# Feed-forward input of a hybrid attention/mLSTM block: one plain step fewer, one seven-product step more, and two weight sums per step formed by accumulating DMA

## The chip, the cores and the metric

The kernel runs on one core of a Trainium2 chip, in fp32 kept exact enough by splitting. The metric is device time in microseconds (us) of one execution; a run is given as the median of its executions. TensorE (PE) multiplies, VectorE (DVE) and ScalarE (ACT) do elementwise work and empty PSUM, GpSimd (POOL) does small work and issues DMAs in software, SyncE (SP) issues most DMAs.

## The reference

Two layers on 512 tokens of width 1024: a dilated attention mixer and an mLSTM mixer, each followed by a SwiGLU feed-forward. The change is in the feed-forward's first half, run once per layer:

```python
def swiglu(xn, w_in, w_out):
    gu = xn @ w_in
    return (jax.nn.silu(gu[..., :D_FF]) * gu[..., D_FF:]) @ w_out
```

`xn` is the RMS-normalized activation, 512 x 1024; `w_in` is 1024 x 5632 (gate and up, D_FF = 2816 columns each); `w_out` is 2816 x 1024.

## The kernel before

**Split products.** TensorE takes operands in a reduced format (float32r). Each fp32 operand is split into a high half, rounded by ACT (`split_chunk`, line 208), and a low half, the remainder, by DVE (line 209). Each product is then three matmuls (`SPLITS`: high-high, high-low, low-high).

**Steps.** `ffn_in` works through the 2816 hidden columns in eleven steps of 256 (j = 0, 2, ..., 20), each step making gate and up of its columns for all 512 tokens. There are two kinds.

A plain step (`plain`, `multiply`, line 239) multiplies four weight chunks of 512 x 256 in the usual way: 96 matmuls that are 512 wide. The normalization factor is multiplied in when PSUM is emptied (line 959).

A product step (`weights_of`, `products`, line 1017) uses a seven-product scheme in the manner of Strassen and Winograd. The weights of a step are four blocks, A11 and A12 (gate, first and second half of the input rows) and A21 and A22 (up), 512 KB each; the tokens are blocks B11 to B22 of the normalized input. From them come the sums S1 to S4 (weights) and T1 to T4 (tokens), and seven products of 256 x 512 x 256 replace eight: `PRODUCTS` lists them in order. Each is 24 matmuls that are 256 wide, so a step has 168. The token sums are made once per layer by the generator `normalized` and kept as split tiles; `some(n)` runs its next n pieces. The weight sums are made in each step by DVE (`total`, line 988) when a block has been split (`prepare`, line 992):

```python
                if key == "A11":
                    total("S1", "A21", "A22", ALU.add, "own")
                elif key == "S1":
                    total("S2", "S1", "A11", ALU.subtract, "own")
                elif key == "S2":
                    total("S3", "A11", "A21", ALU.subtract, "A21")
                elif key == "A12":
                    total("S4", "A12", "S2", ALU.subtract, "A12")
```

S1 and S2 share one buffer (tag `t1`), S3 overwrites A21, S4 overwrites A12.

**Buffers and order.** Splitting runs two products ahead of TensorE (`AHEAD`). Split halves have three buffers each (`whi`, `wlo`), A22 and A12 three (`wraw`), A11 and A21 lie together in a tile of tag `w8` with two buffers; the two `w8` buffers first hold the normalized tokens. A scheduler sets the order of instructions on each engine and the waits by data and buffer dependence; an engine and a DMA queue take their instructions in that order, so an instruction that waits holds up all behind it. All weight loads are issued from SP (line 980). Pool issues nothing in this stage.

In the trace the stage's tiles are named `f0...` and `f1...` by layer; buffer numbers are left out, so `f0j8S` is the S1 and S2 buffer of step j8 and `f0j10A` its neighbour's A blocks; `f0j_w` is a `w8` tile. `_h` and `_l` are the high and low halves.

Of the kernel before, what the change touches and what calls it, by code (L numbers as in the profile page):

```python
# [11 lines left out]
F32 = mybir.dt.float32  # L12
# [3 lines left out]
ALU = mybir.AluOpType  # L16
AX = mybir.AxisListType
P = 128

SEQ = 512  # L20
# [50 lines left out]
def tile_hybrid_dilated_attn_mlstm(  # L71
# [4 lines left out]
    nc = tc.nc  # L76
# [268 lines left out]
    with ExitStack() as actx:  # L345
# [16 lines left out]
        ang, n, sn, cs = (tmp[:, 0, i * P:(i + 1) * P] for i in range(4))  # L362
# [430 lines left out]
        def out_project(pairs, w2d, nk, name, first=0, end=KC // 2):  # L793
            for c in range(first, end):
# [4 lines left out]
        acc = [[acc_tile("awo0_%d" % m) for m in range(2)],  # L799
               [ps.tile([P, 512], F32, tag="s", name="awo1_%d" % m, bufs=2) for m in range(2)],  # L800
               [acc_tile("awo2_0"), ps.tile([P, 512], F32, tag="t", name="awo2_1", bufs=1)]]
# [51 lines left out]
    HALF = SEQ // 2  # L853

    PRODUCTS = (("A11", "B11"), ("S1", "T1"), ("S2", "T2"), ("A12", "B21"), ("S3", "T3"), ("S4", "B22"), ("A22", "T4"))
    PLAIN = 6
    AHEAD = 2

    def ffn_in(layer, fp, pair, rbc, hook, following):
# [11 lines left out]
        def place(i, name, dtype):  # L871
            p, tag = (xp, "x%d" % (i - 3)) if 3 <= i < 11 else (fp, "hid%d" % i)
            return p.tile([P, 2, SEQ], dtype, tag=tag, name="f%d%s%d" % (layer, name, i))
# [1 line left out]
        def hidden(i):  # L875
            return place(i, "hid", F32)

        def temp(tag, name, bufs=1):
            return fp.tile([P, SEQ], F32, tag=tag, name=name, bufs=bufs)

        def op_tile(i, name):
            return fp.tile([P, 4, HALF], F32R, tag="op%d" % i, name="f%d%s" % (layer, name))
# [4 lines left out]
        def split_tokens(key):  # L887
            i = [b for _, b in PRODUCTS].index(key)
            hi, lo = ops[key] = [op_tile(2 * i + part, key + "hl"[part]) for part in range(2)]
            nc.scalar.activation(hi, raw[key], AF.Copy)  # L890
            nc.vector.tensor_tensor(lo, raw[key], hi.bitcast(F32), op=ALU.subtract)

        def normalized():
            xs = [fp.tile([P, 4, SEQ], F32, tag="w8", name="f%dx%d" % (layer, i), bufs=2) for i in range(2)]
            for i in range(2):
                for t in range(2):
                    raw["B%d%d" % (i + 1, t + 1)] = xs[i][:, :, t * HALF:(t + 1) * HALF]
            for k in range(KC):
                nc.vector.scalar_tensor_tensor(xs[k // 4][:, k % 4], h[k], col("ffn", layer * KC + k), rbc,
                                               op0=ALU.mult, op1=ALU.mult)  # L900
                yield
            split_tokens("B11")
            raw["T1"] = fp.tile([P, 4, HALF], F32, tag="t1", name="f%dt1" % layer)
            nc.vector.tensor_tensor(raw["T1"], raw["B12"], raw["B11"], op=ALU.subtract)
            yield

            raw["T3"] = raw["B12"]
            nc.vector.tensor_tensor(raw["T3"], raw["B22"], raw["B12"], op=ALU.subtract)
            split_tokens("T1")
            yield  # L910
            split_tokens("T3")
            yield
            split_tokens("B22")
            yield
            raw["T2"] = raw["B22"]
            nc.vector.tensor_tensor(raw["T2"], raw["B22"], raw["T1"], op=ALU.subtract)
            split_tokens("T2")
            yield
            split_tokens("B21")
            yield  # L920

            raw["T4"] = raw["B21"]
            nc.vector.tensor_tensor(raw["T4"], raw["B21"], raw["T2"], op=ALU.subtract)
            split_tokens("T4")

        hid = []
        steps = normalized()
        STEPS = 2

        def some(n):  # L930
            for _ in itertools.islice(steps, n):
                pass
# [10 lines left out]
        def plain(j):  # L943
            nm = "f%dj%d" % (layer, j)
            acc = {(half, m): bank("%s_%d%d" % (nm, half, m)) for half in range(2) for m in range(2)}
            gates = {}
            hid.append(hidden(j // 2))
            for ch in range(KC // 4):
                for half in range(2):
                    whl = ready.pop(0)  # L950
                    split_next()
                    for m in range(2):
                        multiply(acc[half, m], whl, pair, ch, m, KC)
                        if j == 0 and (ch, half, m) == (1, 0, 0):
                            hook()
                    if ch == KC // 4 - 1:
                        for m in range(2):
                            t = temp("gu%d" % half, nm + "gu", 3 - half)
                            nc.vector.tensor_tensor(t, acc[half, m], rbc, op=ALU.mult)
                            if half == 0:  # L960
                                nc.scalar.activation(t, t, AF.Silu)
                                gates[m] = t
                            else:
                                nc.vector.tensor_tensor(hid[-1][:, m], t, gates[m], op=ALU.mult)
                    advance()
                    if j > 0 or ch == 1:
                        some(STEPS)


        def weights_of(j):  # L970

            nm = "f%dj%d" % (layer, j)
            w8 = fp.tile([P, 2, 1024], F32, tag="w8", name=nm + "_w8", bufs=2)
            w = {"A11": w8[:, 0], "A21": w8[:, 1]}
            for key in ("A22", "A12"):
                w[key] = wp.tile([P, 1024], F32, tag="wraw", name=nm + key, bufs=W_BUFS)
            for key in ("A11", "A22", "A12", "A21"):
                half, ch = int(key[1]) - 1, int(key[2]) - 1
                c0 = half * D_FF + j * P
                nc.sync.dma_start(w[key].rearrange("p (k n) -> p k n", k=4),  # L980
                                  wi[ch * 4 * P:(ch + 1) * 4 * P, c0:c0 + 256].rearrange("(k p) n -> p k n", p=P))

            def split(key):
                return split_chunk((w[key], 1024, lambda t: t.rearrange("p (k n) -> p k n", k=4), nm + key))

            def total(key, a, b, op, place):
                w[key] = w[place]
                nc.vector.tensor_tensor(w[key], w[a], w[b], op=op)
            w["own"] = fp.tile([P, 1024], F32, tag="t1", name=nm + "S")
            made = {}  # L990

            def prepare(key):
                made[key] = split(key)

                if key == "A11":
                    total("S1", "A21", "A22", ALU.add, "own")
                elif key == "S1":
                    total("S2", "S1", "A11", ALU.subtract, "own")
                elif key == "S2":
                    total("S3", "A11", "A21", ALU.subtract, "A21")  # L1000
                elif key == "A12":
                    total("S4", "A12", "S2", ALU.subtract, "A12")
            return [(lambda key=key: prepare(key)) for key, _ in PRODUCTS], made

        def products(j, made):
# [44 lines left out]
            def p3():  # L1050
                product("S4", "B22", "p5", fresh=False)
                hid.append(hidden(j // 2))
                t["g2"] = temp("gu0", nm + "g2", 3)
                add(t["g2"], acc["p5"], t["u2"])
                nc.scalar.activation(t["g2"], t["g2"], AF.Silu)
                nc.vector.tensor_tensor(hid[-1][:, :, HALF:], first(t["v5"]), first(t["g2"]), op=ALU.mult)

            def p4():
                product("A22", "T4", "u", fresh=False)
                nc.vector.tensor_tensor(hid[-1][:, :, :HALF], first(acc["u"]), first(t["g1"]), op=ALU.mult)  # L1060
            return [p1, p5, p6, p2, p7, p3, p4]

        split_next()
# [6 lines left out]
        def prepare(n):  # L1070
            if n < len(todo):
                j, i = todo[n]
                if j not in prepared:
                    prepared[j] = weights_of(j)
                prepared[j][0][i]()
            else:
                out_weights.append(following(n - len(todo)))
# [12 lines left out]
                part.append(x)  # L1090
        for n in range(AHEAD):
            prepare(n)
        some(None)
        for n, (j, i) in enumerate(todo):
            prepare(n + AHEAD)
            if i == 0:
                steps_of = products(j, prepared[j][1])
            steps_of[i]()
            if i % 2:
                advance()  # L1100
            if n >= len(todo) - 3:
                split_hidden()
# [305 lines left out]
    with ExitStack() as fctx:  # L1408
# [3 lines left out]
        def load(ch, n):  # L1412
            src = wo[ch * 2 * P:(ch + 1) * 2 * P, n * 512:(n + 1) * 512].rearrange("(k p) n -> p k n", p=P)
            return split_weights(src, [P, 2, 512], "fw%d_%d" % (n, ch))
# [127 lines left out]
```

## Time and profile before

| what | us |
|---|---|
| median of three runs (1428.53 to 1429.28) | 1428.57 |
| profiled execution's own time | 1428.88 |
| its span, first to last instruction | 1427.1 |
| TensorE busy | 1415.9 (99%) |
| DVE busy | 960.4 (67%) |
| ACT busy | 603.4 (42%) |
| Pool busy | 84.8 (6%) |
| feed-forward input, layer 0: three plain steps | 503.7 to 570.4 |
| feed-forward input, layer 0: eight product steps | 570.4 to 731.7 |

The span is one execution taken by the hardware profiler. Busy times of matmuls overlap, since they are pipelined; what a matmul costs is the distance between the starts of two of them. In rows of the windows the columns are the stretch in us, its length, and for each engine its busy time and the number of instructions, then the granted TensorE clock, the share of the DMA engines and GB/s. In rows of the timeline they are start, duration, engine, line, operation, tile written and tiles read, and in brackets the idle time before it with what ended that. In rows of the DMA issues the last number is the median time from issue to landing.

### The profile page before, as it was taken

How to read it: one execution, taken by the hardware profiler on the slowest of the kernel's cores; microseconds unless marked ns; L12 is line 12 of the kernel's file. 1: busy time of each engine (PE TensorE's matmuls, PEld its weight loads, DVE VectorE, ACT ScalarE, POOL GpSimd, SP SyncE). 2: the span in 40 equal slices, each digit the busy share in tenths (PEclk: the TensorE clock that was granted, in tenths of full speed). 3: DMA queues.
4: the chain of work that ended last, by engine and by line, in shares of the span. 5: the costliest groups of instructions: out<-in, count | busy, mean ns of one | idle time of the engine just before them, and what ended most of it. 6: DMA issues, size and time to landing. Idle time of an engine off the chain costs nothing. (4 is left out here: it accounts for less than half of the span.)

```text
span 1427.1 us, 20255 instructions
## 1 busy us (share of the span) xinstructions
PE 1415.9 (99%) x7986; PEld 1241.2 (87%) x7986; DVE 960.4 (67%) x1679; ACT 603.4 (42%) x1009; POOL 84.8 (6%) x137
## 2 busy tenths in 40 slices
PE   9999999999999999999999999999999999999998
PEld 7888888888888888999998888888888899998887
DVE  7857567567567397787782358897758777888233
ACT  5333224224225353444462233696534354445123
POOL 1011011011002000000000010110000000001001
PEclk9999999999999999999999999999999999999999
DMA  6346236235335434323233232321133332346331
GB/s 193 102 115 201 75 104 191 97 108 151 133 104 145 145 101 133 107 72 118 90 96 96 96 98 74 104 60 60 55 113 96 122 118 83 96 118 180 116 106 72
DMA packets 133688, 158.67 MB, mean 111 GB/s; under 512 B 7060, under 2 KB 121044, under 8 KB 133592
## 3 DMA queue, kind: packets, MB, share of 16 engines
q1 hardware_dynamic: 125616, 131.55, 29.6%
q0 software_dynamic: 6320, 24.69, 6.2%
q8 instruction: 63, 1.03, 0.3%
q10 hardware_dynamic: 1656, 1.12, 0.2%
q14 instruction: 33, 0.27, 0.1%
HBM read 143.18 MB, written 14.16 MB: 110 GB/s over the span
## 5 line engine op out<-in xcount | busy, mean ns | idle before, releaser
L1471 PE MATMUL fin<-fw_l,f1hh 128*128 128x512 f32 (+1 forms) x198 | 72.5, 366 | 0.0
L1471 PE MATMUL fin<-fw_h,f1hh 128*128 128x512 f32 (+1 forms) x198 | 72.4, 366 | 0.0
L1471 PE MATMUL fin<-fw_h,f1hl 128*128 128x512 f32 (+1 forms) x198 | 72.4, 365 | 0.0
L209 DVE TENSOR_TENSOR fo_k_l<-fo_k_w,fo_k_h 128x1024 fp32r<-128x1024 f32 (+1 forms) x24 | 27.2, 1135 | 62.0 <-ACT fo_k_h L208 62.0
L239 PE MATMUL fo<-f0hh,fo_k_h 128*128 128x512 f32 x176 | 68.5, 389 | 0.0
L239 PE MATMUL fo<-f0hl,fo_k_h 128*128 128x512 f32 x176 | 68.5, 389 | 0.0
L239 PE MATMUL fo<-f0hh,fo_k_l 128*128 128x512 f32 x176 | 68.5, 389 | 0.0
L209 DVE TENSOR_TENSOR fw_l<-fw_w,fw_h 128x1024 fp32r<-128x1024 f32 x22 | 27.1, 1233 | 59.9 <-ACT fw_h L208 59.9
L208 ACT ACTIVATE fo_k_h<-fo_k_w 128x1024 fp32r<-128x1024 f32 (+1 forms) x24 | 23.7, 989 | 74.7 <-PE fo L239 74.7
L208 ACT ACTIVATE fw_h<-fw_w 128x1024 fp32r<-128x1024 f32 x22 | 23.3, 1060 | 67.6 <-PE fin L1471 67.0
L1471 PEld LDWEIGHTS fin<-fw_l,f1hh 128*128 128x128 f32 x198 | 37.4, 189 | 6.2 <-DVE fw_l L209 0.2
L1471 PEld LDWEIGHTS fin<-fw_h,f1hh 128*128 128x128 f32 x198 | 37.3, 189 | 6.2
L1471 PEld LDWEIGHTS fin<-fw_h,f1hl 128*128 128x128 f32 x198 | 37.3, 188 | 6.0
L239 PEld LDWEIGHTS fo<-f0hh,fo_k_l 128*128 128x128 f32 x176 | 33.0, 188 | 6.9
L239 PEld LDWEIGHTS fo<-f0hl,fo_k_h 128*128 128x128 f32 x176 | 33.0, 188 | 6.9
L239 PEld LDWEIGHTS fo<-f0hh,fo_k_h 128*128 128x128 f32 x176 | 33.0, 188 | 6.7
L239 PE MATMUL f0j<-n_h,f0j_h 128*128 128x512 f32 x96 | 37.5, 390 | 0.0
L239 PE MATMUL f1j<-n_h,f1j_h 128*128 128x512 f32 x96 | 37.5, 390 | 0.0
L239 PE MATMUL f0j<-n_h,f0j_l 128*128 128x512 f32 x96 | 37.4, 389 | 0.0
L239 PE MATMUL f1j<-n_h,f1j_l 128*128 128x512 f32 x96 | 37.4, 389 | 0.0
L239 PE MATMUL f0j<-n_l,f0j_h 128*128 128x512 f32 x96 | 37.3, 389 | 0.0
L239 PE MATMUL f1j<-n_l,f1j_h 128*128 128x512 f32 x96 | 37.3, 389 | 0.0
(2105 smaller groups left out, 4886.0 us busy)
## 6 DMA issues: line engine op xcount, KB each, us to landing
f0j_w<-in_ffn_w_in_dram SPq DMA_DIRECT2D x28, 512.0 KB, 4.9
f1j_w<-in_ffn_w_in_dram SPq DMA_DIRECT2D x28, 512.0 KB, 4.4
fw_w<-in_ffn_w_out_dram SPq DMA_DIRECT2D x22, 512.0 KB, 3.9
fo_k_w<-in_ffn_w_out_dram SPq DMA_DIRECT2D x20, 512.0 KB, 3.5
awo_k_w<-in_attn_w_out_dram SPq DMA_DIRECT2D x8, 512.0 KB, 7.1
mv_k_w<-in_mlstm_w_in_dram SPq DMA_DIRECT2D x8, 512.0 KB, 3.7
mqk_k_w<-in_mlstm_w_in_dram SPq DMA_DIRECT2D x8, 512.0 KB, 3.9
mo_k_w<-in_mlstm_w_in_dram SPq DMA_DIRECT2D x8, 512.0 KB, 3.7
```

The costliest lines, as they stand in the source:

```text
L208: nc.scalar.activation(hi[:, :n], raw[:, :n], AF.Copy)
L209: nc.vector.tensor_tensor(lo[:, :n], raw[:, :n], hi[:, :n].bitcast(F32), op=ALU.subtract)
L239: nc.tensor.matmul(acc, whl[a][:, k, m * P:(m + 1) * P], pairs[b][kk], start=(kk == 0 and (a, b) == SPLITS[0]), stop=(kk == nk - 1 and (a, ...
L1471: nc.tensor.matmul(acc[i][:, cs], a[a_][kk][:, tb * P:(tb + 1) * P], whl[b_][:, k, cs], start=(kk == 0 and (a_, b_) == SPLITS[0]), stop=(k ...
```

## The change

`PLAIN` goes from 6 to 4: each layer has two plain steps (j = 0, 2) and nine product steps (j = 4 to 20).

The signs of the scheme are turned so that every weight sum is an addition, the up blocks counting as negative: S1 = A21 + A22, S2 = S1 + A11, S3 = A11 + A21, S4 = A12 + S2, with T1, T2 and T4 turned to match, and a factor -1 in the last multiplication of a step.

S1 and S3 are no longer made by DVE. SP loads A11 twice, once into its place and once into S3's; Pool loads A21 into S1's buffer and then issues two DMAs that add to what lies there: A22 onto S1, A21 onto S3. S2 and S4 stay on DVE.

The token sums' pieces come in another order; what is left of them after the plain steps runs one piece per product in the first product step. T1 has a tile of its own (`tt`), and the first product step's A11 and S3 lie in two buffers of the normalized input, since the tokens still hold the `w8` tiles.

```diff
-    PLAIN = 6
+    PLAIN = 4
...
-            w8 = fp.tile([P, 2, 1024], F32, tag="w8", name=nm + "_w8", bufs=2)
-            w = {"A11": w8[:, 0], "A21": w8[:, 1]}
+
+            if j == PLAIN:
+                w8 = [place(i, nm + "_w8", F32).rearrange("p a b -> p (a b)") for i in (5, 6)]
+            else:
+                w8 = fp.tile([P, 2, 1024], F32, tag="w8", name=nm + "_w8", bufs=2)
+                w8 = [w8[:, 0], w8[:, 1]]
+            w = {"A11": w8[0], "S3": w8[1], "S1": fp.tile([P, 1024], F32, tag="t1", name=nm + "S")}
             for key in ("A22", "A12"):
                 w[key] = wp.tile([P, 1024], F32, tag="wraw", name=nm + key, bufs=W_BUFS)
-            for key in ("A11", "A22", "A12", "A21"):
-                half, ch = int(key[1]) - 1, int(key[2]) - 1
+
+            def load(key, block, engine, **kw):
+                half, ch = int(block[1]) - 1, int(block[2]) - 1
                 c0 = half * D_FF + j * P
-                nc.sync.dma_start(w[key].rearrange("p (k n) -> p k n", k=4),
-                                  wi[ch * 4 * P:(ch + 1) * 4 * P, c0:c0 + 256].rearrange("(k p) n -> p k n", p=P))
+                engine.dma_start(w[key].rearrange("p (k n) -> p k n", k=4),
+                                 wi[ch * 4 * P:(ch + 1) * 4 * P, c0:c0 + 256].rearrange("(k p) n -> p k n", p=P), **kw)
+            for key, block in (("A11", "A11"), ("S3", "A11"), ("A22", "A22"), ("A12", "A12")):
+                load(key, block, nc.sync)
+
+            load("S1", "A21", nc.gpsimd)
+            load("S1", "A22", nc.gpsimd, accum_op=ALU.add)
+            load("S3", "A21", nc.gpsimd, accum_op=ALU.add)
...
                 made[key] = split(key)
 
-                if key == "A11":
-                    total("S1", "A21", "A22", ALU.add, "own")
-                elif key == "S1":
-                    total("S2", "S1", "A11", ALU.subtract, "own")
-                elif key == "S2":
-                    total("S3", "A11", "A21", ALU.subtract, "A21")
+                if key == "S1":
+                    total("S2", "S1", "A11", "S1")
                 elif key == "A12":
-                    total("S4", "A12", "S2", ALU.subtract, "A12")
+                    total("S4", "A12", "S2", "A12")
...
-                nc.vector.tensor_tensor(hid[-1][:, :, HALF:], first(t["v5"]), first(t["g2"]), op=ALU.mult)
+                nc.vector.scalar_tensor_tensor(hid[-1][:, :, HALF:], first(t["v5"]), -1.0, first(t["g2"]),
+                                               op0=ALU.mult, op1=ALU.mult)
...
-        some(None)
         for n, (j, i) in enumerate(todo):
             prepare(n + AHEAD)
+            some(1)
```

In the changed program Pool's queue holds, step after step: the S3 sum of a later step, the A21 load into the S1 buffer, the A22 accumulation onto it.

More of the change, by code (lines that the diff above doesn't have):

```diff
@@ L876, in hidden, with temp @@
             return place(i, "hid", F32)
-        def temp(tag, name, bufs=1):
-            return fp.tile([P, SEQ], F32, tag=tag, name=name, bufs=bufs)
+        def temp(tag, name, bufs=1, shape=[P, SEQ]):
+            return fp.tile(shape, F32, tag=tag, name=name, bufs=bufs)
         def op_tile(i, name):
@@ L901, in normalized @@
                 yield
+            raw["T1"] = temp("tt", "f%dt1" % layer, shape=[P, 4, HALF])
+            nc.vector.tensor_tensor(raw["T1"], raw["B11"], raw["B12"], op=ALU.subtract)
             split_tokens("B11")
-            raw["T1"] = fp.tile([P, 4, HALF], F32, tag="t1", name="f%dt1" % layer)
-            nc.vector.tensor_tensor(raw["T1"], raw["B12"], raw["B11"], op=ALU.subtract)
             yield
-            raw["T3"] = raw["B12"]
-            nc.vector.tensor_tensor(raw["T3"], raw["B22"], raw["B12"], op=ALU.subtract)
             split_tokens("T1")
             yield
-            split_tokens("T3")
+            raw["T3"] = raw["B11"]
+            nc.vector.tensor_tensor(raw["T3"], raw["B22"], raw["B12"], op=ALU.subtract)
+            raw["T2"] = raw["B12"]
+            nc.vector.scalar_tensor_tensor(raw["T2"], raw["T1"], -1.0, raw["B22"], op0=ALU.mult, op1=ALU.subtract)
             yield
[L913 to L916, printed above, removed]
             split_tokens("T2")
@@ L920, in normalized @@
             yield
+            split_tokens("T3")
             raw["T4"] = raw["B21"]
-            nc.vector.tensor_tensor(raw["T4"], raw["B21"], raw["T2"], op=ALU.subtract)
+            nc.vector.scalar_tensor_tensor(raw["T4"], raw["T2"], -1.0, raw["B21"], op0=ALU.mult, op1=ALU.subtract)
+            yield
+            split_tokens("B22")
+            yield
             split_tokens("T4")
@@ L927, in ffn_in @@
         steps = normalized()
-        STEPS = 2
         def some(n):
@@ L966, in plain, with total @@
                     if j > 0 or ch == 1:
-                        some(STEPS)
+                        some(2)
         def weights_of(j):
             nm = "f%dj%d" % (layer, j)
-            w8 = fp.tile([P, 2, 1024], F32, tag="w8", name=nm + "_w8", bufs=2)
-            w = {"A11": w8[:, 0], "A21": w8[:, 1]}
+            if j == PLAIN:
[4 more added lines that the diff above has]
+            w = {"A11": w8[0], "S3": w8[1], "S1": fp.tile([P, 1024], F32, tag="t1", name=nm + "S")}
             for key in ("A22", "A12"):
                 w[key] = wp.tile([P, 1024], F32, tag="wraw", name=nm + key, bufs=W_BUFS)
-            for key in ("A11", "A22", "A12", "A21"):
-                half, ch = int(key[1]) - 1, int(key[2]) - 1
+            def load(key, block, engine, **kw):
+                half, ch = int(block[1]) - 1, int(block[2]) - 1
                 c0 = half * D_FF + j * P
-                nc.sync.dma_start(w[key].rearrange("p (k n) -> p k n", k=4),
-                                  wi[ch * 4 * P:(ch + 1) * 4 * P, c0:c0 + 256].rearrange("(k p) n -> p k n", p=P))
+                engine.dma_start(w[key].rearrange("p (k n) -> p k n", k=4),
[5 more added lines that the diff above has]
+            load("S3", "A21", nc.gpsimd, accum_op=ALU.add)
             def split(key):
                 return split_chunk((w[key], 1024, lambda t: t.rearrange("p (k n) -> p k n", k=4), nm + key))
-            def total(key, a, b, op, place):
+            def total(key, a, b, place):
                 w[key] = w[place]
-                nc.vector.tensor_tensor(w[key], w[a], w[b], op=op)
-            w["own"] = fp.tile([P, 1024], F32, tag="t1", name=nm + "S")
+                nc.vector.tensor_tensor(w[key], w[a], w[b], op=ALU.add)
             made = {}
@@ L1055, in p3 @@
                 nc.scalar.activation(t["g2"], t["g2"], AF.Silu)
-                nc.vector.tensor_tensor(hid[-1][:, :, HALF:], first(t["v5"]), first(t["g2"]), op=ALU.mult)
+                nc.vector.scalar_tensor_tensor(hid[-1][:, :, HALF:], first(t["v5"]), -1.0, first(t["g2"]),
+                                               op0=ALU.mult, op1=ALU.mult)
             def p4():
                 product("A22", "T4", "u", fresh=False)
-                nc.vector.tensor_tensor(hid[-1][:, :, :HALF], first(acc["u"]), first(t["g1"]), op=ALU.mult)
+                nc.vector.scalar_tensor_tensor(hid[-1][:, :, :HALF], first(acc["u"]), -1.0, first(t["g1"]),
+                                               op0=ALU.mult, op1=ALU.mult)
             return [p1, p5, p6, p2, p7, p3, p4]
```

## The prediction

> **What bounds the kernel now.** I read the page's first part, then the windows of single steps, then the timelines of DVE, ACT and SP inside one step, and last the DMA issues. The page first:
>
> ```profile
> span 1427.1 us, 20255 instructions
> PE 1415.9 (99%) x7986; PEld 1241.2 (87%) x7986; DVE 960.4 (67%) x1679; ACT 603.4 (42%) x1009; POOL 84.8 (6%) x137
> ```
>
> TensorE never rests, so only matmul time can be won, and a wait is paid where it reaches TensorE. Busy time misleads for matmuls: the rows give 389 ns for a 512-wide and 283 ns for a 256-wide one, but their starts lie 0.227 and 0.120 us apart. The windows are cut at the first matmuls of four steps of layer 0: plain j2, plain j4, products j6, products j8 (columns: stretch, length, then busy us and count per engine, granted clock, DMA share, GB/s).
>
> ```profile
> 526.89:548.65 21.76, 21.76 (x97) 18.02 (x96) 21.64 (x24) 11.43 (x12) 0.00 (x0) 1.00 0.49 155
> 548.65:570.41 21.76, 21.76 (x97) 18.02 (x96) 13.21 (x14) 5.40 (x6) 0.00 (x0) 1.00 0.32 102
> 570.41:590.57 20.16, 20.16 (x170) 20.15 (x169) 15.15 (x15) 9.88 (x12) 0.00 (x0) 1.00 0.35 106
> 590.57:610.73 20.16, 20.16 (x171) 20.16 (x170) 15.71 (x16) 9.88 (x12) 0.00 (x0) 1.00 0.34 105
> ```
>
> A plain step is 96 matmuls x 0.2267 = 21.76 us, a product step 168 x 0.120 = 20.16 us, both without a gap. Pool does nothing here.
>
> **What TensorE gains.** Each layer trades one plain step for one product step: 21.76 - 20.16 = 1.60 us, for two layers 3.2 us. That is all there is to win: 0.22% of 1428.6 us, just past the 0.2% (2.86 us) that a measurement of this kernel can tell from no change.
>
> **The edits beside TensorE.** Two DVE sums of 1.23 us leave each product step (S1 and S3), so DVE falls from 15.7 to about 13.3 us of 20.16; no gain, TensorE covers it. The two multiplications by -1 (scalar_tensor_tensor, 0.70 us on line 899 against 0.69 for the plain multiplication) cost nothing for the same reason. Preparing the operands in two plain steps: in the second one DVE is full already (21.64 of 21.76), and now products follow at once. I laid the changed order of DVE's queue on the durations above: low half of A11 ready at 546.1 for a product that starts at 548.65, S1 at 547.1 for 551.5, S2 at 551.4 for 554.4, A12 at 554.3 for 557.3. The A11 of the first product step lands in a buffer of the normalized input that TensorE frees at 537.5, and two loads of 5 us fit before. So this costs nothing; with one DVE operation more in front of S2 it would still fit. SP issues four loads a step as before (a second A11 takes the place of A21).
>
> **The new chain through Pool.** This is where the change can lose. S1 has one buffer (tag t1), in which S2 is formed too and which is read until S4 = A12 + S2 is done. Before, DVE rebuilt S1 right after that, in 1.23 us. Now Pool waits for S4, loads A21 into the buffer, waits for the landing, and adds A22 by a second DMA; behind these in Pool's queue stand the S3 sum of a later step and the next S1. The first row below is S4 of step j8, the others are step j10's S1 split, S2 sum, S2 split, A12 split and S4 sum on DVE:
>
> ```profile
> 595.93 1.23 DVE L988 TENSOR_TENSOR f0j8A<-f0j8A,f0j8S 128x1024 f32<-128x1024 f32 x1
> ...
> 609.02 1.23 DVE L209 TENSOR_TENSOR f0j10S_l<-f0j10S,f0j10S_h 128x1024 fp32r<-128x1024 f32 x1 [0.28 <-ACT f0j10S_h L208]
> ...
> 610.76 1.22 DVE L988 TENSOR_TENSOR f0j10S<-f0j10S,f0j_w 128x1024 f32<-128x1024 f32 x1
> ...
> 613.19 1.23 DVE L209 TENSOR_TENSOR f0j10S_l<-f0j10S,f0j10S_h 128x1024 fp32r<-128x1024 f32 x1 [0.61 <-ACT f0j10S_h L208]
> 614.83 1.23 DVE L209 TENSOR_TENSOR f0j10A_l<-f0j10A,f0j10A_h 128x1024 fp32r<-128x1024 f32 x1 [0.41 <-ACT f0j10A_h L208]
> 616.09 1.22 DVE L988 TENSOR_TENSOR f0j10A<-f0j10A,f0j10S 128x1024 f32<-128x1024 f32 x1
> ```
>
> The ACT half of the S1 split starts the chain; the A12 half waits 0.57 us for a buffer that TensorE frees:
>
> ```profile
> 607.93 1.06 ACT L208 ACTIVATE f0j10S_h<-f0j10S 128x1024 fp32r<-128x1024 f32 x1 [1.82 <-PE f0j_p L1017]
> ...
> 613.74 1.06 ACT L208 ACTIVATE f0j10A_h<-f0j10A 128x1024 fp32r<-128x1024 f32 x1 [0.57 <-PE f0j_c L1017]
> ```
>
> From the S1 split's start to S4's end it is 617.31 - 607.93 = 9.4 us, or 8.9 when the chain is late and that buffer is already free. Call the two DMAs, from issue to landing, together Z. Add 0.4 us for each Pool start (0.3 from DVE's end at 121.35 to Pool's issue at 121.65; 0.55 from a landing to the issue at 136.38) and 0.1 to ACT. One round of the chain is Z + 0.9 + 8.9 = Z + 9.8 us, and it fits into a step while Z is at most 20.16 - 9.8 = 10.36.
>
> The first round has more room. From S4's end at 597.16 to the split at 607.93 there are 10.8 us, and S2's low half, done at 614.42, is wanted at 610.73 + 2 x 2.88 = 616.49: 2.0 us of slack. The first product step's S1 is loaded early. Eight rounds follow in each layer, one with the room of 12.8 and seven that repeat: the loss of a layer is (Z + 0.9 - 12.8) + 7 x (Z - 10.36) = 8Z - 84.4, if positive.
>
> **The size of Z.** No accumulating DMA is in this trace. The nearest issues, in us to landing:
>
> ```profile
> ht<-hD POOLq DMA_DIRECT2D x2, 1024.0 KB, 6.8
> a1pT<-a1pD POOLq DMA_DIRECT2D x2, 960.0 KB, 7.3
> a3pT<-a3pD POOLq DMA_DIRECT2D x2, 960.0 KB, 9.0
> f0j10A<-in_ffn_w_in_dram SPq DMA_DIRECT2D x2, 512.0 KB, 4.8
> f0j12A<-in_ffn_w_in_dram SPq DMA_DIRECT2D x2, 512.0 KB, 6.2
> f0j18A<-in_ffn_w_in_dram SPq DMA_DIRECT2D x2, 512.0 KB, 5.7
> a1v<-a1vD POOLq DMA_DIRECT2D x1, 512.0 KB, 4.3
> ```
>
> The load of A21 has the shape of a1v, also from Pool: 4.3 us with little beside it. In the product steps it competes with SP's loads, which there take 4.8 to 6.2; I take 5.4, between them. The accumulation brings 512 KB and reads 512 KB more; from below it costs a plain load, 4.3, from above the slowest transfer of 960 KB, 9.0. I take 6.8, the row of 1024 KB from Pool's queue, since the doubled read is what it is nearest to. Z = 12.2, between 8.6 and 15.2. A cost below a plain load is excluded: the same 512 KB come from memory.
>
> DMA work is the reason not to take the low end. Four loads make a share of 0.34 of 20.16 us, 1.7 us each; with seven loads and two second reads it is 9 x 1.7 = 15.3 us, a share of 0.76.
>
> **The sum.** 8 x 12.2 - 84.4 = 13.2 us a layer, 26.4 for both, less 3.2: 23.2 us slower. Against the profiled execution's own 1428.88 us (1.78 beside its span of 1427.1; 0.31 above the median of 1428.57) that is 1452.1, against the median 1451.8. I forecast 1452.
>
> **The rivals.** *The chain fits.* With Z up to 10.5 (the accumulation near 5 us) ACT finds S1 landed, TensorE stays the bound, and the two layers give their 3.2 us: 1425.4. For it: a load of this shape takes 4.3 us, and even two of them make 8.6. Against it: the second read and SP's four loads, which fall into the same half of the step (issues at 599.6 to 604.5, S4 done at 597.2). Chance 0.21.
>
> *Late by little.* The second read costs only its transfer: 4.3 + 1.7 = 6.0, Z = 11.4, 6.8 us a layer, 13.6 - 3.2 = 10.4 us slower: 1439. Its low edge, Z from 10.6 to 11.0, is no measurable change. Chance 0.15, of which 0.05 within 0.2%. The Trainium skill, Collectives: The Full Stack, section on the bandwidth ceiling, says that a DMA's add costs no cycles of its own and is slower only because two source reads share one ring. By that the time would be this rival's, 1439, and not 1452; no run here shows an accumulating DMA yet.
>
> *Far later.* The read-modify-write is not pipelined as a copy is, and Z passes 15.2: from 1500 us up (Z = 20 would be 75.6 us a layer, 1577). For it: nothing in this trace shows such a transfer at all. Against it: all plain ones of 512 KB land within 6.2 us. Chance 0.12.
>
> **How the numbers follow.** The forecast, Z from 11.5 to 15.2, has the remaining 0.52. Chances: faster 0.21 (the chain fits), same 0.05 (the low edge of late by little), slower 0.10 + 0.52 + 0.12 = 0.74. The range reaches from the fitting chain, 1425, to Z = 15.2, 1500, and leaves out the far case. The likely cases' own range, without the fitting chain, is 1430 to 1500.
>
> **What would show it.** Right: product steps from the second on longer than 20.16 us, by about 1.8 us each, with ACT's S1 split ending its idle time on a Pool DMA and TensorE idle before S1 or S2 products; the first product step and the plain steps without gaps; Pool's accumulating DMAs landing 6 to 9 us after issue. The chain fits: 20.16 us in every product step and S1 landed before ACT asks. Wrong altogether: gaps in the first product step (operand preparation), or a wait on the S3 sum or on SP's loads in place of S1.

## The result

The changed kernel takes 1479.52 us (median of four runs, 1477.29 to 1482.34) against 1428.91 for the kernel before beside it: 50.6 us more, a ratio of 1.0355, 95% interval 1.0337 to 1.0373. Forecast was 1452. The profiled execution took 1477.29 us.

The head of the page after:

```profile
span 1475.5 us, 20650 instructions
PE 1431.5 (97%) x8130; PEld 1256.6 (85%) x8130; DVE 930.7 (63%) x1653; ACT 609.2 (41%) x1021; POOL 144.8 (10%) x191
```

TensorE is at 97% instead of 99%: for the first time it waits. The windows of layer 0, cut at the first matmuls of the product steps j4, j6, j8 and j10 (columns as before):

```profile
549.00:569.15 20.15, 20.15 (x170) 20.15 (x168) 13.01 (x14) 8.30 (x10) 4.62 (x4) 1.00 0.90 225
569.15:595.05 25.90, 23.37 (x171) 22.88 (x169) 13.35 (x13) 9.75 (x12) 3.37 (x3) 0.87 0.56 139
595.05:618.08 23.03, 20.81 (x170) 20.31 (x169) 13.35 (x13) 9.67 (x12) 3.33 (x3) 1.00 0.64 158
618.08:640.56 22.48, 20.67 (x170) 20.26 (x169) 13.34 (x13) 9.67 (x12) 3.33 (x3) 1.00 0.67 162
```

The first product step has no gap, and the second plain step before it still takes 21.76 us, so the hurried operand preparation costs nothing. From the second product step on every step is late, by 1.5 to 5.7 us in layer 0. DVE has the 13.35 us that were forecast. The nine product steps of a layer take 205.1 and 209.1 us.

The new chain, in the timelines of Pool and ACT between step j8's S4 and step j10's. Pool first: load of A21 onto S1, accumulation of A22, the S3 accumulation of another step, the next S1:

```profile
606.31 0.78 POOL L985 DMA_DIRECT2D f0j10S<-in_ffn_w_in_dram  x1 [13.59 <-DVE f0j8A L999]
611.04 1.27 POOL L985 DMA_DIRECT2D f0j10S<-in_ffn_w_in_dram  x1 [3.95 <-DMA f0j10S<-in_ffn_w_in_dram]
614.22 1.27 POOL L985 DMA_DIRECT2D f0j_w<-in_ffn_w_in_dram  x1 [1.91 <-DMA f0j_w<-in_ffn_w_in_dram]
628.79 0.78 POOL L985 DMA_DIRECT2D f0j12S<-in_ffn_w_in_dram  x1 [13.29 <-DVE f0j10A L999]
```

```profile
619.36 1.06 ACT L208 ACTIVATE f0j10S_h<-f0j10S 128x1024 fp32r<-128x1024 f32 x1 [5.89 <-DMA f0j10S<-in_ffn_w_in_dram]
```

In brackets stand the idle time before each instruction and what ended it. Pool waits 13.59 us for DVE's S4 sum; ACT, which found S1 ready before, now waits 5.89 us for the accumulation to land. In most late steps TensorE then waits in the product of S1 and again before that of S2, here in j8 (the rows of its timeline that have an idle time):

```profile
599.25 0.39 PE L1023 MATMUL f0j_p<-f0T1h,f0j8S_l 128*128 128x256 f32 x1 [0.76 <-DVE f0j8S_l L209]
...
603.59 0.39 PE L1023 MATMUL f0j_u<-f0T2h,f0j8S_h 128*128 128x256 f32 x1 [1.46 <-ACT f0j_u L1035]
```

The first wait is for the low half of S1. The second is for a copy on ACT, which stands behind the late splits in ACT's queue.

Z is the time of the load and the accumulation together, from issue to landing, as in the prediction. The DMA lines of two tiles tell its size. Each has two issues, so the minimum is the load and the maximum the accumulation; first f0j4S, the S1 of the first product step, loaded before the stage, then f0j10S:

```profile
DMA to landing us min/median/max: 4.0/5.1/6.3
...
DMA to landing us min/median/max: 4.4/6.3/8.2
```

Over the 16 late rounds of both layers the load takes 4.77 us on average and the accumulation 8.62 (7.0 to 9.8). The rest of a round is as forecast: 8.88 us from the S1 split to S4's end in every round, and 0.93 us of hand-offs in most.

What the DMA engines do during three accumulations, windows from issue to landing of the S1 accumulations of j4, j10 and j12:

```profile
487.24:493.53 6.29, 6.29 (x29) 5.22 (x28) 3.58 (x5) 3.12 (x5) 1.33 (x1) 1.00 0.57 85
611.04:619.25 8.21, 8.21 (x71) 8.21 (x70) 3.41 (x4) 1.09 (x2) 2.55 (x2) 1.00 1.14 279
633.28:642.93 9.65, 9.65 (x83) 9.65 (x82) 3.65 (x4) 1.33 (x2) 2.55 (x2) 1.00 1.15 269
```

The last two numbers of a row are the DMA share and GB/s. The early accumulation is nearly alone. In the late ones the share is over 1, so the engines are full: SP's loads of A22 and A12 and Pool's S3 accumulation lie in the same stretch. Averaged over the step the share is only 0.6 to 0.7, which hides this.

### The profile page after: what moved, and what is told of

The parts are those of the page before. It is cut to its first block, busy times and chain, and to the rows that moved or that the text cites. A ratio compares the mean times of both kernels' runs of the same rounds, so it can differ in the third digit from the quotient of the medians.

```text
span 1475.5 us, 20650 instructions
## 1 busy us (share of the span) xinstructions
PE 1431.5 (97%) x8130; PEld 1256.6 (85%) x8130; DVE 930.7 (63%) x1653; ACT 609.2 (41%) x1021; POOL 144.8 (10%) x191
## 5 line engine op out<-in xcount | busy, mean ns | idle before, releaser
L538 DVE TENSOR_TENSOR rot<-rot,sinr 32x1024 f32<-32x1024 f32 x24 | 28.9, 1205 | 0.0
L239 PE MATMUL mo<-n_h,mo_k_h 128*128 128x512 f32 x64 | 25.5, 399 | 0.0
L239 PE MATMUL mo<-n_h,mo_k_l 128*128 128x512 f32 x64 | 25.2, 394 | 0.0
L239 PE MATMUL mo<-n_l,mo_k_h 128*128 128x512 f32 x64 | 25.1, 393 | 0.0
L239 PE MATMUL mqk<-n_h,mqk_k_h 128*128 128x512 f32 x64 | 25.1, 393 | 0.0
L239 PE MATMUL mqk<-n_l,mqk_k_h 128*128 128x512 f32 x64 | 25.1, 392 | 0.0
```

The source lines that it names most:

```text
L239: nc.tensor.matmul(acc, whl[a][:, k, m * P:(m + 1) * P], pairs[b][kk], start=(kk == 0 and (a, b) == SPLITS[0]), stop=(kk == nk - 1 and (a, ...
L538: nc.vector.tensor_tensor(sh, sh, sinr.unsqueeze(1).to_broadcast([R, 2, SEQ]), op=ALU.mult)
```

## The experiments

The theory: the loss is the chain through the one S1 buffer, whose round is Z + 9.8 us, and Z is too long. The rivals: the DMA work by itself, the two-step operand preparation, and the lower granted clock in j6 (0.87 above). A gap is, here and below, the distance between the starts of two matmuls of TensorE where it is more than the usual 0.120 us.

**Both sums back on DVE.** The two plain steps alone are kept:

```diff
-            for key, block in (("A11", "A11"), ("S3", "A11"), ("A22", "A22"), ("A12", "A12")):
+            for key, block in (("A11", "A11"), ("S3", "A21"), ("A22", "A22"), ("A12", "A12")):
...
-            load("S1", "A21", nc.gpsimd)
-            load("S1", "A22", nc.gpsimd, accum_op=ALU.add)
-            load("S3", "A21", nc.gpsimd, accum_op=ALU.add)
...
+                if key == "A11":
+                    total("S1", "S3", "A22", "S1")
...
+                elif key == "S2":
+                    total("S3", "A11", "S3", "S3")
```

> One part of the change alone: two plain steps and nine product steps, but both weight sums back on DVE (SP loads A21 in S3's place; S1 = A21 + A22 and S3 = A11 + A21 are DVE sums, no Pool DMA in the product steps). Theory A (the whole loss is the chain S4, load, accumulation, S1 through Pool): every product step 20.15 us and plain steps 21.76, one plain step for one product step in each layer, 1428.9 - 3.2 = 1425.7 us. Theory B (preparing the operands in two plain steps also costs something that the late sums hid in the changed kernel): gaps in the first product step or in the second plain step, 1427 us or more. Theory C (the load on DVE: 15.7 us of 20.16 a step already before) would give gaps in all product steps, over 1430 us.

Measured 1426.47 us (11 runs) against 1429.29, ratio 0.9981 (0.9972 to 0.9990): 2.8 us faster, where 3.2 were expected. Windows of its first two product steps:

```profile
548.21:568.36 20.15, 20.15 (x169) 20.15 (x168) 18.96 (x20) 10.83 (x13) 0.00 (x0) 1.00 0.49 157
568.36:588.52 20.16, 20.16 (x170) 20.16 (x169) 15.85 (x16) 9.88 (x12) 0.00 (x0) 1.00 0.34 105
```

No gap, even with DVE at 18.96 us in the first. Only in the last product step of layer 1 is there a small one, of 0.87 us, that the kernel before does not have; it is more than the 0.4 us that are missing, which lie within the interval. The traded step and the operand preparation are what the prediction said; theories B and C fall.

**Two places for S1.** The same DMAs and bytes as the changed kernel, but S1 alternates between the `t1` and `tt` places:

```diff
-"S1": fp.tile([P, 1024], F32, tag="t1", name=nm + "S")
+"S1": fp.tile([P, 1024], F32, tag="tt" if (j - PLAIN) % 4 else "t1", name=nm + "S")
```

> All of the changed kernel, but S1's buffer alternates between two places (the t1 place and the place of T1, free by then): same DMAs, same bytes, same accumulations, only the reuse is one step later. Theory A (the wait for the one buffer, not the DMA work): a round of load and accumulation has two steps, 40.3 us, against Z of 13.4 plus 9.8, so no gaps: 1425.7 us. Rival 1 (the accumulating DMAs are too slow or too many for the queue or the memory): S1 accumulation 7.0 to 9.8 plus load 4.4 plus S3 accumulation 8 us follow one another in Pool's queue, about 20 to 22 us a step: 1428 to 1455 us, with the gaps at S1 or S3. Rival 2 (only the first round's queue order, S3 of j8 ahead): gain of some 10 us alone, 1470.

Measured 1426.35 us, ratio 0.9981 (0.9972 to 0.9990). Windows of its first three product steps:

```profile
549.05:569.20 20.15, 20.15 (x170) 20.15 (x168) 14.88 (x16) 9.88 (x12) 4.65 (x4) 1.00 1.07 254
569.20:589.36 20.16, 20.16 (x171) 20.16 (x169) 13.53 (x14) 9.89 (x12) 3.32 (x3) 1.00 0.76 184
589.36:609.52 20.16, 20.16 (x171) 20.16 (x169) 13.53 (x14) 9.88 (x12) 3.34 (x3) 1.00 0.75 185
```

The DMAs are hardly quicker (Z is 13.1 us on average against 13.4, accumulations 6.9 to 9.6), the share is the 0.76 that was estimated, and no step of layer 0 is late (in layer 1 only the last, by 0.69 us, with the small gap of the run above). So the wait for the buffer is the whole loss of 53 us, and the DMA work costs nothing by itself. This kernel and the one with both sums on DVE are the two that beat the kernel before.

**S1's accumulation alone undone.** Pool still loads A21 into the one buffer, DVE adds A22:

```diff
-            load("S1", "A22", nc.gpsimd, accum_op=ALU.add)
...
+                if key == "A11":
+                    total("S1", "S1", "A22", "S1")
...
```

> S1's accumulating DMA alone undone: Pool still loads A21 into the one S1 buffer after S4, but A22 is added there by DVE (1.23 us); S3 is still an accumulating DMA. Theory A (the chain's length decides, and the accumulation of 7.0 to 9.8 us is the piece that is too long): a round is 0.55 + 4.4 + 0.1 + 1.23 + 8.9 = 15.2 us, below the step of 20.16, so all product steps 20.15 us, 1425.7. Rival (the traffic of Pool's accumulations holds up the loads, wherever they are): S3's accumulation still in every step, loads of 5.5 to 6.5 us, steps of 20.5 to 22, 1432 to 1455. In both the S3 accumulation shows its time to landing with one accumulation less in the queue: under 7 us if the two held each other up, near 8 if it is its own cost beside SP's loads.

Measured 1431.30 us, ratio 1.0013 (1.0004 to 1.0021). Theory A's 1425.7 is missed by 5.6 us, though the chain now fits: rounds are 20.16 us in most steps. The gaps (1.1 to 1.6 us, two in a layer, beside the small one at the end of layer 1) come from DVE's queue, here its timeline in step j8:

```profile
597.94 1.23 DVE L209 TENSOR_TENSOR f0j8S_l<-f0j_w,f0j8S_h 128x1024 fp32r<-128x1024 f32 x1
604.17 1.23 DVE L998 TENSOR_TENSOR f0j10S<-f0j10S,f0j10A 128x1024 f32<-128x1024 f32 x1 [5.01 <-DMA f0j10S<-in_ffn_w_in_dram]
605.32 1.22 DVE L209 TENSOR_TENSOR f0j8S_l<-f0j8A,f0j8S_h 128x1024 fp32r<-128x1024 f32 x1
```

The sum waits 5.01 us for Pool's load, and the low half of S4, which TensorE wants, stands behind it. S3's accumulations took 7.2 us on average, between the two values expected.

**S3's accumulation alone undone.**

```diff
-            for key, block in (("A11", "A11"), ("S3", "A11"), ("A22", "A22"), ("A12", "A12")):
+            for key, block in (("A11", "A11"), ("S3", "A21"), ("A22", "A22"), ("A12", "A12")):
...
-            load("S3", "A21", nc.gpsimd, accum_op=ALU.add)
...
+                elif key == "S2":
+                    total("S3", "A11", "S3", "S3")
```

> S3's accumulating DMA alone undone (SP loads A21 in S3's place, DVE adds A11 after S2; SP's and Pool's loads are one fewer), S1 still by load and accumulation in one buffer, so the chain stays. If S1's accumulation of 8.6 us (mean) is its own cost: Z 13.0, steps from the second product on about 22.8 us, 1470 to 1478 us. If it is slowed by S3's accumulation and its load in the same time: accumulation near the 6.1 to 6.3 us that it takes alone in the first product step's S1, Z = 4.4 + 6.2 = 10.6, a loss of 8 x 10.6 - 84.4 = 0.4 us a layer: 1426 to 1432 us. Between: the share of each, 8 us a layer for 1 us of Z.

Measured 1478.75 us, ratio 1.0345 (1.0331 to 1.0359): no gain. S1's accumulation still takes 8.63 us on average. Here is the window of j10's accumulation from issue to landing:

```profile
610.85:619.07 8.22, 7.77 (x65) 7.60 (x64) 3.82 (x5) 1.06 (x1) 1.28 (x1) 1.00 0.96 239
```

In the changed kernel the same accumulation took 8.21 us at a share of 1.14. So the second accumulation in the same time is not what makes it long, and the share in the stretch alone does not give the time.

**A plain load in the accumulation's place.**

```diff
-            load("S1", "A22", nc.gpsimd, accum_op=ALU.add)
+            load("S1", "A22", nc.gpsimd)
```

> The chain of the changed kernel with the same two DMAs in one S1 buffer, but the second is a plain load of A22 in place of the accumulation (the sum S1 lacks A21; S3 is still accumulated). If the accumulation's own read-modify-write is what makes Z too long: the second DMA lands in 4.3 to 5.4 us, as the first does, Z = 4.4 + 4.9 = 9.3, under 10.36, only the first round late: 1425.7 to 1430 us. Rival (any second DMA behind a landing, in the midst of SP's four loads, takes 8 us): no change, 1475 to 1480 us.

Measured 1446.58 us, ratio 1.0130 (1.0108 to 1.0152), between the two expectations. Windows from issue to landing of the second load, first in the early one of j4, then j10 and j12:

```profile
487.43:491.44 4.01, 4.01 (x20) 3.31 (x19) 1.46 (x3) 1.01 (x2) 0.76 (x1) 1.00 0.42 131
608.60:615.04 6.44, 6.44 (x56) 6.44 (x56) 3.39 (x4) 1.07 (x2) 2.06 (x2) 1.00 1.07 339
629.32:635.06 5.74, 5.74 (x50) 5.74 (x50) 3.40 (x4) 1.08 (x2) 2.07 (x2) 1.00 1.08 348
```

Set beside the windows of the changed kernel these take Z apart. Early and nearly alone, a plain second load takes 4.0 us and an accumulation 6.3 (layer 0, one of each). Among the step's other transfers the plain load takes 6.54 us on average and the accumulation 8.62. So the addition costs 2.1 to 2.3 us in these two places, and the crowd in the step 2.3 to 2.5. In the early place of layer 1, where loads of SP lie beside both, it is only 0.7; first the plain load, then the accumulation of the changed kernel:

```profile
1049.34:1054.76 5.42, 5.42 (x26) 4.48 (x25) 1.31 (x2) 1.06 (x1) 0.74 (x1) 1.00 0.59 196
1064.26:1070.36 6.10, 6.10 (x29) 5.05 (x28) 1.92 (x2) 1.17 (x2) 1.31 (x1) 1.00 0.89 181
```

Of the 53 us between the changed kernel and the one with two places for S1, the addition makes 33 (1479.5 - 1446.6); two plain loads in this place would still cost 20.

**One of SP's loads taken out.** The last product takes A11 where A22 belongs:

```diff
-            for key in ("A22", "A12"):
-                w[key] = wp.tile([P, 1024], F32, tag="wraw", name=nm + key, bufs=W_BUFS)
+            w["A22"] = w["A11"]
+            w["A12"] = wp.tile([P, 1024], F32, tag="wraw", name=nm + "A12", bufs=W_BUFS)
...
-            for key, block in (("A11", "A11"), ("S3", "A11"), ("A22", "A22"), ("A12", "A12")):
+            for key, block in (("A11", "A11"), ("S3", "A11"), ("A12", "A12")):
```

> The changed kernel without SP's load of A22 (the last product takes A11 in its place; the sum S1 still accumulates the real A22): three of SP's four loads are left in each step, the chain stays. If S1's accumulation is at 8.6 us because SP's loads are beside it (6.1 to 6.3 us alone), a quarter of the surplus of 2.4 us goes with a quarter of the loads: Z 0.6 us less, 8 x 0.6 = 4.8 us a layer, 1470 us; more if A22's load was the one beside it. If the accumulation's time is its own whenever TensorE and the other engines work: 1477 to 1480 us.

Measured 1453.93 us, ratio 1.0173 (1.0156 to 1.0190), 26 us less than with the load. The accumulation falls to 7.25 us on average, the load to 4.48. From issue to landing of j10's and j12's accumulation:

```profile
607.62:614.18 6.56, 6.56 (x57) 6.56 (x56) 3.84 (x4) 1.57 (x3) 1.27 (x1) 1.00 1.00 226
628.10:635.27 7.17, 7.17 (x62) 7.17 (x62) 3.76 (x4) 1.44 (x2) 1.27 (x1) 1.00 0.94 219
```

The accumulation is 1.4 us shorter, of the 2.3 us of crowding. But more than the load of A22 has changed. POOL has one instruction in these windows instead of two: S3's accumulation now comes later, which by the run with S3 on DVE is worth nothing alone. And SP's other loads lie at other times:

```profile
606.10 0.37 SPq L985 DMA_DIRECT2D f0j14A<-in_ffn_w_in_dram  x1
608.93 0.98 SPq L985 DMA_DIRECT2D f0j_w<-in_ffn_w_in_dram  x2
```

The two loads into the `w8` buffer are issued 1.3 us after the accumulation (607.62), where the changed kernel issues them 4.1 us before it (606.92 against 611.04). So the run shows that SP's loads lengthen Pool's accumulation, but not what the load of A22 is worth by itself.

**A place of its own for the second product step's S1 alone.**

```diff
-tag="t1", name=nm + "S")
+tag="tt" if j == PLAIN + 2 else "t1", name=nm + "S")
```

> The changed kernel, but the S1 of the second product step (j6) alone has a place of its own. The j6 and j8 steps then have no late chain, and six rounds (j10 to j20) are left in each layer, the first with the 12.8 us of room. By the formula of the prediction with the measured Z of 13.2: (13.2 + 0.9 - 12.8) + 5 x (13.2 - 10.36) = 15.5 us a layer, 1425.7 + 31 = 1457 us, if the waits for S1 are all there is to it and no gap is long enough to bring the lower granted clock that followed the gaps of 2.3 us in j6. Rival (the first round is just the place where a loss shows that the DMA work makes in any case): the gap of 2.3 us and the slow matmuls move to j8 or j10, 1470 us or more.

Measured 1459.88 us, ratio 1.0213 (1.0197 to 1.0228), 3 us over the formula. Windows of j10 and j12:

```profile
609.48:630.01 20.53, 20.41 (x171) 20.21 (x169) 13.35 (x13) 9.01 (x12) 3.32 (x3) 1.00 0.67 171
630.01:653.74 23.73, 20.93 (x170) 20.32 (x169) 13.35 (x13) 9.67 (x12) 3.34 (x3) 1.00 0.63 154
```

The first late step is j10 as expected, and by 0.37 us only: the room before the first round is real. From j12 on the rounds repeat. The clock stays at 1.00: in neither layer does a stretch of slow matmuls follow a gap. The loss without the clock is the loss of the chain.

**TensorE gaps without Pool.** Extra DVE operations in the kernel with both sums on DVE:

```diff
                     total("S2", "S1", "A11", "S1")
+                    for _ in range({8: 3, 12: 4, 16: 5, 20: 6}.get(j, 0)):
+                        nc.vector.tensor_tensor(w["A11"], w["A11"], w["A11"], op=ALU.max)
```

> The kernel with both sums on DVE (no Pool DMA in the product steps), with extra DVE operations of 1.23 us between S2's sum and its split: three in j8, four in j12, five in j16, six in j20, which with the 2.0 us of slack make one TensorE gap of about 1.7, 2.9, 4.2 and 5.4 us. If a gap over about 2 us by itself brings the lower granted clock (in the changed kernel's j6 24 to 27 matmuls 0.213 us apart instead of 0.120, 2.2 to 2.5 us): none after 1.7, some 25 slow matmuls after each of the other three, steps of 21.9, 25.4, 26.6, 27.9 us, 1426 + 28 + 14 = 1468 us. If the low clock belongs to the accumulating DMAs' traffic: spacing 0.120 after every gap, 1454 us.

Measured 1467.88 us (one run). Windows of j12 and j16 in layer 0, then j12 in layer 1:

```profile
630.43:653.16 22.73, 20.75 (x170) 20.33 (x169) 21.10 (x21) 9.89 (x12) 0.00 (x0) 1.00 0.28 92
673.32:700.49 27.17, 23.21 (x170) 22.71 (x169) 22.15 (x22) 9.99 (x12) 0.00 (x0) 0.87 0.25 79
1216.19:1240.42 24.23, 22.25 (x170) 21.83 (x169) 21.10 (x21) 9.88 (x12) 0.00 (x0) 0.93 0.27 88
```

The low clock comes with no Pool DMA in sight, so the gap brings it. The gaps fell before S3, not S2, and were 1.27, 1.82, 4.09 and 6.36 us. After 1.27 no matmul is slow, after 4.09 and 6.36 some are in both layers. After 1.82 none are in layer 0 and 15 in layer 1, which is the 1.5 us between the first and third row. The time agrees with the expected 1468 partly by chance: 94 slow matmuls make 94 x 0.093 = 8.8 us, less than the 14 expected, and the gaps make about 33 instead of 28.

## Why the prediction was wrong in size

**TensorE's gain, the edits, the operands: right.** 3.2 us forecast, 2.8 measured by the two kernels without the wait (interval 1.4 to 4.0); no gap in the first product step. The small gap at the end of layer 1 was not foreseen.

**The chain: right in place, weights and hand-offs.** Pool waits for S4, ACT waits for Pool's accumulation, 8.88 us against 8.9 and 0.93 against 0.9. The signs that were named came, but for their size: steps from the second on late, ACT's S1 split freed by a Pool DMA, TensorE idle before S1 and S2, accumulations in 6 to 9 us (9.8 at most). The steps are longer by about 3.2 us on average, not 1.8.

**Z: the step that failed.** The forecast took 5.4 us for the load and 6.8 for the accumulation, Z = 12.2. Measured are 4.77 (4.5 without the two rounds of j6, where the S3 accumulation lies beside it) and 8.62: the load was taken 0.6 us too long and the accumulation 1.8 us too short. Z is 13.20 in layer 0 and 13.56 in layer 1. In 8Z this is 8.0 + 10.9 = 18.9 us of the 24 us by which the loss was too small: the span of the kernel with two places for S1, 1425.0, and the changed one's of 1475.5 are 50.5 us apart, and the forecast had 26.4. Two choices were behind it. The row of 1024 KB from Pool's queue (6.8 us) was taken for the doubled read; nearly alone the accumulation takes 6.0 to 6.3, so the row was near that, but it is from another stretch of the kernel, and the crowding was added to the load instead. The load of j10 is issued at 606.31, just ahead of SP's first two (606.92 and 607.34), and takes 4.4 us all the same. The accumulation, 4.7 us later, runs beside what is left of these, SP's A12 and A22 (609.04 and 611.87) and S3's accumulation. And the crowding was weighed with a DMA share of 0.76 over the whole step, where the stretch itself has 1.14. Even that does not give the time: at shares of 0.96 and 1.00 j10's accumulation took 8.2 us with S3 on DVE and 6.6 without the load of A22. What decides how the transfers share the engines stays open.

**What is left**, some 5 us, is in two small terms. The hand-offs of a round were a little slower than 0.9 us, most of all in layer 0's first rounds (the load of j6 was issued 1.02 us after S4 instead of 0.55): 1.15 us a layer. And of the slack of 2.0 us that was credited to the first round, which is worth 1.5 us a layer in the formula (84.4 against 8 x 10.36 = 82.9), nearly nothing could be kept: from S4's end in the last step to the end of the stage TensorE needs 13.16 and 14.30 us, against 13.58 and 14.27 without the late chain.

**The clock: not part of the loss.** In the changed kernel 24 matmuls of layer 0 and 55 of layer 1 start 0.213 us apart. But the rounds of the chain account for the whole loss: from S4 of j4 to S4 of j20 layer 0 takes 185.15 us, of which Z is 105.6 and the split and sums 8 x 8.88 = 71.0; the 8.5 left are hand-offs. While the chain is late TensorE waits anyway, and slow matmuls only fill the wait.

**The rivals.** *The chain fits* argued that even two plain loads make 8.6 us; in their place they make 11.4, and cost 20 us. *Late by little* took 6.0 us for the accumulation. The Trainium skill, Collectives: The Full Stack, section on the bandwidth ceiling, says of a reduce-scatter that it is slower not because the add costs cycles but because it needs two source reads. For the accumulation nearly alone the trace agrees with this rival's size: 6.0 to 6.3 us against 4.0 for the plain load, near its 6.0. Whether the second read or the add makes the difference, no run here separates. It did not give the time, for the crowd added as much again. Another page bears on that: the Trainium skill, DMA: Bandwidth & Descriptors, section on issuing engines, says that DMAs of all issuers run on the same engines and interleave. The trace agrees: with one load fewer in SP's queue, and the others at other times, Pool's accumulation took 1.4 us less.

## What to carry to other kernels

When a sum moves from an engine into a DMA, ask what its buffer has to wait for: 1.23 us of DVE work in a single buffer became 14.3 us of hand-offs and transfers in the same place, and a second place made it free. Take a transfer's time from the stretch in which it will run, with the transfers that lie beside it there, not from a row elsewhere and not from a share of the engines alone. And an engine in order that is made to wait for a DMA holds back all that is queued behind it, as DVE did with S4's low half.

## What the runs showed of the hardware

An accumulating DMA of 512 KB from memory onto SBUF lands 6.0 to 6.3 us after issue with little beside it (layer 0's first one, in five kernels), where one plain load took 4.0 us. Among the step's transfers it takes 8.6 on average against 6.5. Its instruction takes Pool 1.27 us instead of 0.78.

Gaps of TensorE can bring a lower granted clock: 256-wide matmuls then start 0.213 us apart instead of 0.120, for some 2 to 6 us. It came every time after a gap of 2.3 to 6.4 us, which shorter ones followed closely, and after 1.82 us, with 0.72 close behind, in one of two cases. In the changed kernel's layer 1 it came after two gaps of 0.99 and 1.04 us close together, while 0.83 and 1.04 us in layer 0 left the clock alone, as did the lone gaps of up to 1.74 us there. The Trainium skill, TensorE: Matmul & The Clock Gate, Part 1, tells of a gate that watches windows of about 3.4 us, free-running, so that the same kernel can show different counts; the varying answer to one gap of 1.82 us agrees with that, but gaps below 3.4 us were enough here.
